# c as eight packed columns that TensorE spreads, and a column of ones that ties the first tiles' work behind the first dot

## The chip, the cores and the metric

The kernel runs on one core of one Trainium2 chip, in one launch. A core has five engines that run their own instruction streams: TensorE (PE in the rows, with its weight loads as PEld), VectorE (DVE), ScalarE (ACT), GpSimd (POOL) and SyncE (SP, which here issues most DMAs). They are held together by semaphores: an instruction waits until what it reads is written and what it overwrites has been read. The metric is the device time of one execution in microseconds (us), smaller is better.

## The reference

The model is a trunk of two mixer layers, each followed by a gated MLP with a width-3 convolution, on 1024 tokens of 1024 channels in f32. Every sub-layer is normalised and modulated by a vector that is computed from one conditioning row c of 1024 numbers. Cut to what the change touches:

```python
c_act = jax.nn.silu(c)
for i in range(DEPTH):
    mod = c_act @ mod_w[i] + mod_b[i]
    sh_a, sc_a, g_a, sh_f, sc_f, g_f = [t[:, None, :] for t in jnp.split(mod, 6, axis=-1)]
    h = rms_norm(x) * (1 + sc_a) + sh_a
    ...
        proj = h @ w_in
        cq, ckv, k_rope = jnp.split(proj, [512, 768], axis=-1)
```

So nothing of the first projection can be multiplied before the scales (1 + sc_a) of its channels are there, and these are dot products of silu(c) with 1024 rows of mod_w.

## The kernel before, in words

Everything is stored with channels on the 128 partitions: x is eight tiles k of 128 channels by 1024 tokens, and the tokens are worked on in two halves of 512. Every f32 matrix product is made of three reduced-precision ones: each operand is split into a high part (ScalarE copies it to the narrower type) and a low part (VectorE subtracts), and `mm3` (L171) multiplies the weight's high part by that of x (L175), the weight's high by x's low (L176) and the weight's low by x's high (L177). In the profile's rows the first operand behind the arrow is the moving one.

The change lies in the first stage, the input projection of the first half. Its inner dimension is the eight channel tiles k. For each k three things are loaded: 128 rows of mod_w (tile `sraw`, 512 KB), 128 rows of the projection weight (tile `wraw`, 448 KB) and a tile of x (256 KB); `load_k` issues the three, and `load_x` the last. `prepare(k)` then does, in this order: VectorE's dot of the mod_w rows with the row `crow` (`mod_dot`, L198, which writes one column of `modc`), the bias on that column (`mod_bias`, L203), ScalarE's high part of the weight (`winh`, L339), the high part of x times the scale column (`scaled`, L347, tile `h`), VectorE's low part of the same (L348), and the low part of the weight (`winl`, L341). `in_k` lets TensorE multiply the tile into seven PSUM accumulators `ia`, 21 matmuls for each k, 168 in all. Beside it ScalarE squares each x tile (L236, L239) and VectorE adds the squares (L241); after the last tile TensorE sums them over partitions (`st`, L250), VectorE makes the variance (`var`, L254), GpSimd the power -0.5 (`rstd`, L255), and TensorE spreads the result over rows (`rb`, L262). The accumulators are read out with that result.

`crow` is silu(c) on all 128 partitions. Before, a DMA writes c to every partition (L134, 128 rows of 4 KB) and ScalarE applies Silu to the 128x1024 tile (L135). Constants that are needed as columns lie packed in `cols`, 124 columns in its first part, loaded by one DMA (L156) in `load_k(0)`. Until the first real matmul TensorE runs 14 matmuls of 128x128 on the identity (`warm`, L405); each is shown as two records.

In the same stage stand the tables for the rotary embedding (`rope_tables`: four small loads of the positions into the tile `rt`, seventeen small operations on ScalarE and VectorE), further dots with loaded rows (`row`, the tiles `row` of mod_w), and the loads and splits of the second half of x.

The order of the instructions on each engine is not the order of the source: a scheduler of the framework orders them ahead of time from the program, its dependences and its own estimates, except where `tc.high_priority()` or `tc.keep_in_program_order` stand. So an edit at the start can shift what stands where on each engine in the first stage; the order below shows where.

## Time and profile before

| | us |
|---|---|
| three runs | 2194.0, 2195.18, 2199.16 |
| median of the three | 2195.18 |
| the profiled execution, its own time | 2196.67 |
| span of that execution in the trace | 2194.9 |
| TensorE busy | 2164.6 (99%) |
| VectorE busy | 1692.5 (77%) |
| ScalarE busy | 1049.7 (48%) |
| mean granted TensorE clock | 0.994 |

Times in the trace count from the start of the span. The span is from the first to the last instruction that the profiler records; 1.77 us of the execution lie around it. Matmuls are pipelined, so the busy time of TensorE counts a matmul as busy from its start to its modelled end; the granted clock tells how fast it was allowed to run (1.00 is 2.4 GHz, 0.50 is 1.2 GHz). In a row of the timeline the bracket tells how long the engine had stood idle before the instruction and what it waited for. Idle time of an engine that nobody waits for costs nothing.

### The profile page before, as it was taken

What the parts mean: (1) busy time and instruction counts of PE and PEld (TensorE: products, weight loads), DVE (VectorE), ACT (ScalarE), POOL (GpSimd) and SP (SyncE); (2) the same over time, 40 slices, a digit from 0 to 9 for tenths busy, and PEclk for the clock granted to TensorE, in tenths of its full rate; (3) what the DMA queues carried; (4) which work ended last, traced back from release to release, by engine and by line L of the source; (5) the groups of instructions that cost most, each with busy time, mean ns of one, the idle gap of its engine ahead of it and who ended that gap; (6) DMA issues with size and microseconds to landing.
All of it is one profiled execution on the core that took longest, in us unless ns stands there. A gap on an engine that the chain in (4) does not pass through costs nothing.

```text
span 2194.9 us, 28739 instructions
## 1 busy us (share of the span) xinstructions
PE 2164.6 (99%) x10557; PEld 1818.9 (83%) x10557; DVE 1692.5 (77%) x2769; ACT 1049.7 (48%) x1812; POOL 175.2 (8%) x216
## 2 busy tenths in 40 slices
PE   9999999999999999999999999999999999999998
PEld 7878888787888888878888888988788888887887
DVE  8877878669878777899973655566897777779997
ACT  6465566446544444443454434354554444453335
POOL 0000000000000000042210111010000000002232
PEclk9999999999999999999999999999999999999999
DMA  8512334831444332642132233444243333245122
GB/s 317 151 51 62 93 105 146 284 129 68 158 139 136 124 123 92 206 151 88 53 122 92 59 125 115 130 151 176 68 144 101 111 109 103 72 158 194 64 80 77
DMA packets 105085, 270.50 MB, mean 123 GB/s; under 512 B 12336, under 2 KB 15984, under 8 KB 104944
## 3 DMA queue, kind: packets, MB, share of 16 engines
q1 hardware_dynamic: 104544, 268.28, 37.2%
q8 instruction: 83, 1.36, 0.3%
q14 instruction: 58, 0.48, 0.1%
q10 hardware_dynamic: 400, 0.39, 0.1%
HBM read 221.53 MB, written 44.47 MB: 121 GB/s over the span
## 4 chain that ended last, share of the span: by engine, by line
PE 84%; DVE 9%; DMA 2%; ACT 2%; issue 2%; POOL 0%; SPq 0%; DVEq 0%; POOLq 0%; ACTq 0%
PE pa L175 7%; PE pa L177 7%; PE pa L176 7%; PE sc L673 3%; PE pd L177 3%; PE pd L175 3%; PE pd L176 3%; PE db L175 3%; PE db L176 3%; PE db L177 3%; PE op L175 3%; PE op L176 3%; PE op L177 3%; PE da L175 2%; PE da L176 2%; PE da L177 2%
## 5 line engine op out<-in xcount | busy, mean ns | idle before, releaser
L988 ACT ACTIVATE whi<-raw 128x512 fp32r<-128x512 f32 (+1 forms) x252 | 147.9, 608 | 248.3 <-PE pb L176 61.0
L988 ACT ACTIVATE whi<-wsum 128x512 fp32r<-128x512 f32 (+1 forms) x224 | 134.3, 619 | 177.4 <-PE pa L176 61.5
L175 PE MATMUL pa<-T,whi 128*128 128x512 f32 x528 | 205.9, 390 | 0.0
L176 PE MATMUL pa<-T,whi 128*128 128x512 f32 x528 | 205.4, 389 | 0.0
L177 PE MATMUL pa<-T,wlo 128*128 128x512 f32 x528 | 205.1, 389 | 0.0
L989 DVE TENSOR_TENSOR wlo<-wsum,whi 128x512 fp32r<-128x512 f32 (+1 forms) x224 | 151.5, 692 | 33.0 <-ACT whi L988 31.6
L989 POOL TENSOR_TENSOR wlo<-raw,whi 128x512 fp32r<-128x512 f32 (+1 forms) x80 | 116.3, 1467 | 401.2 <-ACT whi L988 398.7
L177 PE MATMUL da<-U,wlo 128*128 128x512 f32 (+1 forms) x364 | 138.4, 383 | 2.0 <-DVE wlo L989 2.0
L175 PE MATMUL da<-U,whi 128*128 128x512 f32 (+1 forms) x364 | 139.3, 383 | 0.4 <-DVE x L294 0.4
L176 PE MATMUL da<-U,whi 128*128 128x512 f32 (+1 forms) x364 | 139.2, 382 | 0.0
L989 DVE TENSOR_TENSOR wlo<-raw,whi 128x512 fp32r<-128x512 f32 (+1 forms) x172 | 116.1, 681 | 24.9 <-ACT whi L988 24.9
L167 ACT ACTIVATE whi<-wraw 128x1024 fp32r<-128x1024 f32 x67 | 70.8, 1060 | 117.5 <-PE op L176 59.3
L175 PEld LDWEIGHTS pa<-T,whi 128*128 128x128 f32 x528 | 99.1, 188 | 22.4 <-ACT whi L988 1.2
L177 PEld LDWEIGHTS pa<-T,wlo 128*128 128x128 f32 x528 | 99.1, 188 | 20.6
L176 PEld LDWEIGHTS pa<-T,whi 128*128 128x128 f32 x528 | 99.1, 188 | 20.2
L1028 ACT ACTIVATE ct<-a,cols 128x512 f32<-128x512 f32 x88 | 71.1, 812 | 83.7 <-DVE a L1050 47.8
L1140 DVE TENSOR_TENSOR U<-q,U 128x1024 fp32r<-128x1024 f32 x84 | 102.7, 1239 | 10.3 <-ACT U L1139 9.8
L168 DVE TENSOR_TENSOR wlo<-wraw,whi 128x1024 fp32r<-128x1024 f32 x67 | 81.7, 1222 | 29.8 <-ACT whi L167 27.7
L175 PE MATMUL db<-U,whi 128*128 128x512 f32 x264 | 103.3, 391 | 1.3 <-ACT whi L988 1.3
L177 PE MATMUL db<-U,wlo 128*128 128x512 f32 x264 | 102.8, 389 | 0.0
L176 PE MATMUL db<-U,whi 128*128 128x512 f32 x264 | 102.8, 389 | 0.0
L175 PE MATMUL inp<-h,whi 128*128 128x512 f32 x256 | 100.9, 395 | 0.0
(378 smaller groups left out, 6079.4 us busy)
## 6 DMA issues: line engine op xcount, KB each, us to landing
raw<-in_wf SPq DMA_DIRECT2D x96, 512.0 KB, 4.1
wraw<-in_w SPq DMA_DIRECT2D x67, 512.0 KB, 3.6
mraw<-in_mod_w SPq DMA_DIRECT2D x56, 512.0 KB, 3.9
ud<-ct SPq DMA_DIRECT2D x88, 256.0 KB, 2.3
q<-ud SPq DMA_DIRECT2D x88, 256.0 KB, 4.3
raw<-in_wd SPq DMA_DIRECT2D x32, 512.0 KB, 6.0
pa<-in_mod_w SPq DMA_DIRECT2D x24, 512.0 KB, 3.7
x<-xd SPq DMA_DIRECT2D x48, 256.0 KB, 4.7
```

The lines of the kernel that those rows point to most:

```text
L167: act.activation(hi, raw, AF.Copy)
L168: dve.tensor_tensor(lo, raw, hi.bitcast(F32), ALU.subtract)
L175: pe.matmul(ps, lh, rh, start=first, stop=False, skip_group_check=more)
L176: pe.matmul(ps[:, 0:rl.shape[-1]], lh, rl, start=False, stop=False, skip_group_check=more)
L177: pe.matmul(ps, ll, rh, start=False, stop=last, skip_group_check=more)
L673: pe.matmul(ps[:, cs], a[:, qs if n < 3 else qrs_], b[:, cs], start=n == 0, stop=n == 4)
L988: act.activation(hi, src, AF.Copy)
L989: eng.tensor_tensor(lo, src, hi.bitcast(F32), ALU.subtract)
L1028: act.activation(t, a[:, 2:], AF.Identity, bias=col(f"cb{l}", m), scale=cw(m, 2))
L1140: dve.tensor_tensor(lo, w, hi.bitcast(F32), ALU.subtract)
```

## The change

The broadcast load of c and the Silu on 128x1024 go. c is stored as eight columns of 128 in `cols`, which thereby has 132 columns in its first part, and that load is now the first one issued. ScalarE applies Silu to the eight columns (`ccol`); TensorE transposes each column, read as 128 equal columns, with the identity, four into one PSUM tile `cr` and four into another; VectorE copies the two tiles into the halves of `crow`, at high priority. The warming matmuls become 4 before the transposes and 5 after them. The first x tile is issued by ScalarE's queue instead of SyncE's. `load_k(0)`, `load_k(1)` and `prepare(0)` now stand ahead of `rope_tables` in the source.

`one` is a column of 128 ones that VectorE computes as 0 times the first scale column plus 1, so it exists only after the first dot and its bias. It is given as the scalar operand of the dots k = 1 to 3, as the scale of the high parts of the weight k = 1 to 3 and of the squares k = 0 to 3, and it is copied into the tile that the positions are loaded into, ahead of their loads. No value changes by it. The low part of the first weight tile is kept in program order.

```diff
@@ -40,7 +40,7 @@
 
 STEPS = "nspppnspppoooonmooso", "nnsposppooponpmspoopo"
 XW = (4, 2)
-WARM = 14
+WARM, WARM2 = 4, 5
 W0, W0_RSTD, WF, WF_RSTD = (6, 10), (4, 3), (4, 5), (4, 4)
 SHARE = 7
 GATES = (2, 18, 22, 26)
@@ -61,7 +61,7 @@
 
 
 
-_W = [("mb0", 48), ("mb1", 48), ("qn", 4), ("kvn", 2), ("hn", 8), ("fn", 8), ("invf", 1), ("mg", 3), ("gb", 2),
+_W = [("mb0", 48), ("mb1", 48), ("qn", 4), ("kvn", 2), ("hn", 8), ("fn", 8), ("invf", 1), ("mg", 3), ("gb", 2), ("c", 8),
       ("cw0", 66), ("cb0", 22), ("cw1", 66), ("cb1", 22)]
 COL = {}
 _o = 0
@@ -131,8 +131,6 @@
 
 
     crow = cst.tile([P, D], F32, name="crow")
-    nc.sync.dma_start(crow, c_d.broadcast_to([P, D]))
-    act.activation(crow, crow, AF.Silu)
     cols = [cst.tile([P, COLS[0][1]], F32, name="cols"), None, None]
     ident = cst.tile([P, P], F32, name="ident")
     make_identity(nc, ident)
@@ -194,8 +192,8 @@
             e[1]()
 
 
-    def mod_dot(l, i, raw, c=None):
-        return dve.scalar_tensor_tensor(raw, raw, 1.0, crow if c is None else c, ALU.mult, ALU.mult, accum_out=modc[l][:, i:i + 1])
+    def mod_dot(l, i, raw, c=None, one=1.0):
+        return dve.scalar_tensor_tensor(raw, raw, one, crow if c is None else c, ALU.mult, ALU.mult, accum_out=modc[l][:, i:i + 1])
 
     def mod_bias(l, i, n=1):
 
@@ -318,7 +316,7 @@
     us = [[(p0w if k < INNER else p0).tile([P, 896], F32R, name=f"win{j}{k}") for j in "hl"] for k in range(KT)]
 
     def load_x(hf, k):
-        nc.sync.dma_start(xs[hf][:, k, :], xT[k, :, hf * HS:(hf + 1) * HS])
+        (act if hf + k == 0 else nc.sync).dma_start(xs[hf][:, k, :], xT[k, :, hf * HS:(hf + 1) * HS])
 
     def small(name):
         return psS.tile([P, HS], F32, tag="sm", bufs=1, name=nm(name))
@@ -326,19 +324,21 @@
     def load_k(k):
 
         nc.sync.dma_start(sraw[:, k % 4, :], mod_w[0, 8 + k])
-        if k == 0:
-            load_cols(0, cst)
         nc.sync.dma_start(wraw[:, k % 4, :], win[k])
         load_x(0, k)
 
     def prepare(k):
         hi, lo = us[k]
         raw = wraw[:, k % 4, :]
-        mod_dot(0, 8 + k, sraw[:, k % 4, :])
+        mod_dot(0, 8 + k, sraw[:, k % 4, :], one=one if 0 < k < 4 else 1.0)
         mod_bias(0, 8 + k)
-        act.activation(hi, raw, AF.Copy)
+        act.activation(hi, raw, AF.Copy, scale=one if 0 < k < 4 else 1.0)
+        if k == 0:
+            dve.tensor_scalar(one, modc[0][:, 8:9], 0.0, 1.0, ALU.mult, ALU.add)
         scaled(0, k)
-        dve.tensor_tensor(lo, raw, hi.bitcast(F32), ALU.subtract)
+        i = dve.tensor_tensor(lo, raw, hi.bitcast(F32), ALU.subtract)
+        if k == 0:
+            tc.keep_in_program_order(i)
 
     def scaled(hf, k):
 
@@ -362,6 +362,7 @@
 
         Q = S // 4
         ang, n, n1, n2, t, pi = [scr[:, i * Q:(i + 1) * Q] for i in range(6)]
+        dve.tensor_copy(pi[:, 0:1], one)
         pi = pi.bitcast(I32)
         for i in range(4):
             nc.sync.dma_start(pi[32 * i:32 * i + 32, :], pos[:, i * Q:(i + 1) * Q].broadcast_to([32, Q]))
@@ -400,19 +401,33 @@
         rstd_later(ssq[hf], D, ssq[hf], keep_rb, XW[hf], small)
 
 
+    load_cols(0, cst)
+    load_k(0)
+    load_k(1)
     ps = small("warm")
     for _ in range(WARM):
         pe.matmul(ps[:, 0:P], ident, ident, start=True, stop=True)
 
-
-    load_k(0)
-    load_k(1)
+    ccol = cst.tile([P, KT], F32, name="ccol")
+    act.activation(ccol, cols_at(COL["c"], KT), AF.Silu)
+    for i in range(2):
+        cr = mm_tile("cr")
+        for t in range(4):
+            pe.transpose(cr[:, t * P:(t + 1) * P], ccol[:, i * 4 + t:i * 4 + t + 1].to_broadcast([P, P]), ident)
+        with tc.high_priority():
+            dve.tensor_copy(crow[:, i * HS:(i + 1) * HS], cr)
+    for _ in range(WARM2):
+        pe.matmul(ps[:, 0:P], ident, ident, start=True, stop=True)
+
+    one = cst.tile([P, 1], F32, name="one0")
+    prepare(0)
+
+
     cs_d = rope_tables(block(1, [P, 6 * 256], F32, "rt"))
     load_k(2)
     load_k(3)
-    prepare(0)
     accA = in_acc()
-    ssq[0].add(xs[0][:, 0, :])
+    ssq[0].add(xs[0][:, 0, :], scale=one)
 
     rows, shrow, inb = [], None, cst.tile([P, 7], F32, name="inb")
 
@@ -460,7 +475,7 @@
             h[1] = [block(4 + i, [P, KT, HS], F32R, "h") for i in range(2)]
             scaled(1, 0)
         if k < KT - 1:
-            ssq[0].add(xs[0][:, k + 1, :])
+            ssq[0].add(xs[0][:, k + 1, :], scale=one if k < 3 else 1.0)
         for r in ROWS_A[k]:
             row(r)
         if k == KT - 2:
@@ -1717,6 +1732,7 @@
     invf = np.array(INVF, f)
     put("invf", np.tile(invf, 4)[:, None])
     put("mg", np.tile(np.array([[MAGIC, -MAGIC, math.pi / 2]], f), (P, 1)))
+    put("c", _cols(a["c"][0]))
     put("gb", np.repeat(a["ml_b_gates"][0].reshape(2, MH).T, NC, axis=0))
 
     wi = a["mla_w_in"][0]
```

TensorE at the program's start. Names with a number are tiles; `ia` are accumulators, `warm` the warming matmuls, `cr` the spread c. Before:

```order
L405 MATMUL warm_116<-ident 128x128 x14
L175 MATMUL ia_174<-h_94,winh_98 128x512
L176 MATMUL ia_174<-h_95,winh_98 128x512
L177 MATMUL ia_174<-h_94,winl_99 128x512
L175 MATMUL ia_175<-h_94,winh_98 128x512
```

and now:

```order
L409 MATMUL warm_121<-ident 128x128 x4
L416 MATMUL cr_128<-ident,ccol 128x128 x4
L416 MATMUL cr_134<-ident,ccol 128x128 x4
L420 MATMUL warm_121<-ident 128x128 x5
L173 MATMUL ia_184<-h_92,winh_96 128x512
L173 MATMUL ia_185<-h_92,winh_96 128x512
L173 MATMUL ia_186<-h_92,winh_96 128x512
```

Before, the first accumulator gets its three products, then the second its three; now the high-by-high product comes first for one accumulator after another. Behind the rows shown there are seven of them in all before the others follow; L173, L174 and L175 now are L175, L176 and L177 of before.

ScalarE at the program's start, `x` with its number being the first half of x and `winh` with different numbers those of k = 0, 1, 2. Before:

```order
L135 ACT_TABLE_LOAD
L135 ACTIVATE crow<-crow 128x1024
L339 ACTIVATE winh_98<-wraw_97 128x896
L347 ACTIVATE h_94<-x_93,modc_79 128x512
L236 ACTIVATE ssq_114<-x_93 128x512
L339 ACTIVATE winh_100<-wraw_97 128x896
L347 ACTIVATE h_94<-x_93,modc_79 128x512
L239 ACTIVATE sq_195<-x_93 128x512
L368 ACTIVATE rt_138<-rt_138,cols 128x256
```

and now:

```order
L319 DMA x_91<-in_xT 128x512
L412 ACT_TABLE_LOAD
L412 ACTIVATE ccol<-cols 128x8
L335 ACTIVATE winh_96<-wraw_95 128x896
L347 ACTIVATE h_92<-x_91,modc_77 128x512
L234 ACTIVATE ssq_112<-x_91,one_145 128x512
L335 ACTIVATE winh_98<-wraw_95,one_145 128x896
L237 ACTIVATE sq_205<-x_91,one_145 128x512
L335 ACTIVATE winh_100<-wraw_95,one_145 128x896
L347 ACTIVATE h_92<-x_91,modc_77 128x512
L237 ACTIVATE sq_238<-x_91,one_145 128x512
```

The tile numbers of the two builds differ by two: the second tile's `winh_100` of before is `winh_98` now, and `winh_100` now is the third tile's. The squares of the second tile and the weight's high part of the third now stand ahead of the second `h`, where before the second `h` came directly behind the second `winh`. The first rotary operation (`rt_138`) stood ninth in the first piece, and it stands behind the rows shown in the second.

VectorE ahead of the first variance (`var`). `h_459` and `h_469` belong to the second half of x (`x_291`, `x_301`), `ssq_115` are the squares of that half, `row_310` to `row_314` dots with rows of mod_w. Before:

```order
L348 SCALAR_TENSOR_TENSOR h_459<-x_291,modc_79,h_458 128x512
L348 SCALAR_TENSOR_TENSOR h_95<-x_93,modc_79,h_94 128x512
L348 SCALAR_TENSOR_TENSOR h_459<-x_291,modc_79,h_458 128x512 x3
L241 TENSOR_TENSOR ssq_115<-ssq_115,sq_582 128x512
L241 TENSOR_TENSOR ssq_115<-ssq_115,sq_585 128x512
L348 SCALAR_TENSOR_TENSOR h_459<-x_291,modc_79,h_458 128x512
L241 TENSOR_TENSOR ssq_115<-ssq_115,sq_588 128x512
L254 TENSOR_SCALAR var_438<-st_433 128x4
```

and now:

```order
L239 TENSOR_TENSOR ssq_112<-ssq_112,sq_412 128x512
L196 SCALAR_TENSOR_TENSOR row_310,modc_77<-row_310,crow 128x1024
L348 SCALAR_TENSOR_TENSOR h_93<-x_91,modc_77,h_92 128x512
L201 SCALAR_TENSOR_TENSOR modc_77<-modc_77,cols 128x1
L196 SCALAR_TENSOR_TENSOR row_312,modc_77<-row_312,crow 128x1024
L196 SCALAR_TENSOR_TENSOR row_314,modc_77<-row_314,crow 128x1024
L201 SCALAR_TENSOR_TENSOR modc_77<-modc_77,cols 128x1
L348 SCALAR_TENSOR_TENSOR h_469<-x_301,modc_77,h_468 128x512
L252 TENSOR_SCALAR var_448<-st_443 128x4
```

Before, five low parts and three sums of squares of the second half stand ahead of the variance in the rows shown; now three dots on rows with two biases, one such low part, and the rest behind it.

## Rows read from the trace of the kernel before

**Rows 1.** The page, first part: busy time of each engine, its share of the span, and its instructions.
```profile
PE 2164.6 (99%) x10557; PEld 1818.9 (83%) x10557; DVE 1692.5 (77%) x2769; ACT 1049.7 (48%) x1812; POOL 175.2 (8%) x216
```

**Rows 2.** Busy time by stretch, whole core. Columns: the stretch, its length, then for PE, PEld, DVE, ACT and POOL the busy time and instructions, then the granted TensorE clock (1.00 is full), the DMA engines' busy share, and GB/s.
```profile
0.00:10.00 10.00, 6.01 (x29) 5.78 (x29) 2.45 (x5) 4.39 (x5) 0.78 (x8) 0.99 0.79 274
10.00:20.00 10.00, 9.72 (x30) 7.38 (x30) 8.71 (x17) 8.33 (x15) 0.00 (x0) 0.67 1.04 380
20.00:40.00 20.00, 20.00 (x90) 16.57 (x89) 19.70 (x37) 12.69 (x22) 0.00 (x0) 1.00 0.82 291
40.00:60.00 20.00, 19.95 (x97) 16.14 (x96) 19.09 (x38) 8.79 (x15) 1.85 (x1) 1.00 0.83 308
```

**Rows 3.** The timeline of the first 13 us. Columns: start in us, length in us, engine, line, operation, output<-input, shapes, count, and in brackets how long the engine had stood idle and what released it.
```profile
1.46 5.69 PE L405 MATMUL warm<-ident 128*128 128x128 f32 x28 [1.46 <-POOL ident masks.py:199]
...
5.08 1.06 ACT L135 ACTIVATE crow<-crow 128x1024 f32<-128x1024 f32 x1 [3.01 <-DMA crow<-in_c]
6.74 1.23 DVE L198 SCALAR_TENSOR_TENSOR sraw<-sraw,crow 128x1024 f32<-128x1024 f32 x1 [6.74 <-DMA sraw<-in_mod_w]
...
7.96 0.95 ACT L339 ACTIVATE winh<-wraw 128x896 fp32r<-128x896 f32 x1 [1.81 <-DMA wraw<-in_win]
...
8.90 0.72 ACT L347 ACTIVATE h<-x,modc 128x512 fp32r<-128x512 f32 x1
...
9.68 0.79 PE L175 MATMUL ia<-h,winh 128*128 128x512 f32 x1 [2.54 <-ACT h L347]
9.95 0.75 DVE L348 SCALAR_TENSOR_TENSOR h<-x,modc,h 128x512 fp32r<-128x512 f32 x1
...
10.75 0.79 PE L176 MATMUL ia<-h,winh 128*128 128x512 f32 x1 [0.28 <-DVE h L348]
...
11.34 0.63 PE L177 MATMUL ia<-h,winl 128*128 128x512 f32 x1
...
11.44 0.95 ACT L339 ACTIVATE winh<-wraw 128x896 fp32r<-128x896 f32 x1 [1.29 <-DMA wraw<-in_win]
...
11.77 0.63 PE L175 MATMUL ia<-h,winh 128*128 128x512 f32 x1
...
12.61 0.73 ACT L347 ACTIVATE h<-x,modc 128x512 fp32r<-128x512 f32 x1 [0.22 <-DMA x<-in_xT]
```

**Rows 4.** Half-microsecond stretches of the start, columns as in rows 2.
```profile
2.00:2.50 0.50, 0.50 (x5) 0.50 (x4) 0.00 (x0) 0.08 (x1) 0.00 (x0) 1.00 0.87 319
6.50:7.00 0.50, 0.50 (x6) 0.45 (x5) 0.26 (x1) 0.00 (x0) 0.00 (x0) 1.00 1.09 376
9.50:10.00 0.50, 0.32 (x1) 0.29 (x1) 0.50 (x2) 0.50 (x2) 0.00 (x0) 0.72 0.97 390
16.50:17.00 0.50, 0.50 (x4) 0.42 (x3) 0.08 (x1) 0.50 (x2) 0.00 (x0) 0.96 0.96 384
```

**Rows 5.** The timeline where the first normaliser is made, columns as in rows 3.
```profile
44.64 0.94 PE L250 MATMUL st<-ones,ssq 128*128 128x1 f32 x8
...
45.62 0.16 DVE L254 TENSOR_SCALAR var<-st 128x4 f32<-128x4 f32 x1 [0.36 <-PE st L250]
...
45.94 1.85 POOL L255 TENSOR_TENSOR rstd<-var,nhalf 128x4 f32<-128x4 f32 x1 [44.53 <-DVE var L254]
...
47.85 0.65 PE L262 MATMUL rb<-ident,rstd 128*128 128x128 f32 x4
```

**Rows 6.** Groups of VectorE's instructions in the first 46 us: line, engine, operation, shapes, count | busy us, mean ns of one | idle time just before them and what ended it.
```profile
L198 DVE SCALAR_TENSOR_TENSOR sraw<-sraw,crow 128x1024 f32<-128x1024 f32 x8 | 9.8, 1222 | 6.7 <-DMA sraw<-in_mod_w 6.7
L348 DVE SCALAR_TENSOR_TENSOR h<-x,modc,h 128x512 fp32r<-128x512 f32 x13 | 9.6, 748 | 0.7 <-ACT h L347 0.7
L341 DVE TENSOR_TENSOR winl<-wraw,winh 128x896 fp32r<-128x896 f32 x8 | 8.7, 1089 | 1.2 <-ACT winh L339 1.2
L241 DVE TENSOR_TENSOR ssq<-ssq,sq 128x512 f32<-128x512 f32 x10 | 6.9, 687 | 0.1
...
L374 DVE TENSOR_TENSOR rt<-rt 128x256 f32<-128x256 f32 x1 | 0.4, 426 | 0.8 <-ACT rt L373 0.8
...
L254 DVE TENSOR_SCALAR var<-st 128x4 f32<-128x4 f32 x1 | 0.2, 164 | 0.4 <-PE st L250 0.4
```

**Rows 7.** The same for ScalarE, two of its groups.
```profile
L347 ACT ACTIVATE h<-x,modc 128x512 fp32r<-128x512 f32 x15 | 10.6, 718 | 3.7 <-DVE modc L203 2.9 <-DMA x<-in_xT 0.8
...
L239 ACT ACTIVATE sq<-x 128x512 f32<-128x512 f32 x12 | 7.3, 618 | 1.9 <-DMA x<-in_xT 1.9
```

**Rows 8.** DMA issues of the first 40 us: output<-input, queue, operation, count, KB each, median us from issue to landing.
```profile
crow<-in_c SPq DMA_DIRECT2D x1, 512.0 KB, 4.3
...
cols<-in_cols SPq DMA_DIRECT2D x1, 62.0 KB, 5.1
```

**Rows 9.** TensorE's waits in the stretch with its largest loss of time (timeline, columns as in rows 3), and behind them two stretches of it (columns as in rows 2).
```profile
112.82 0.50 PE L175 MATMUL qrp<-cqn,whi 128*128 128x512 f32 x1 [0.61 <-ACT cqn L495]
113.93 0.50 PE L176 MATMUL qrp<-cqn,whi 128*128 128x512 f32 x1 [0.61 <-DVE cqn L496]
...
116.59 0.79 PE L175 MATMUL kp<-ckvn,whi 128*128 128x512 f32 x1 [1.93 <-ACT ckvn L495]
...
116.00:118.00 2.00, 1.41 (x5) 1.29 (x6) 1.30 (x3) 1.75 (x3) 0.00 (x0) 0.50 0.52 117
...
122.00:124.00 2.00, 2.00 (x11) 1.83 (x10) 0.72 (x4) 0.00 (x0) 0.00 (x0) 0.91 0.00 0
```

## The prediction

> **What bounds the kernel now.** I read the page's first part before anything else [rows 1]: TensorE is busy 99% of the span, 2164.6 of 2194.9 us, so some 30 us in all are left in which it stands. The change touches only the start, so the next views are the busy times by stretch and the timeline of the first microseconds [rows 2, 3]. The reader is to see there what the start costs TensorE: 1.46 us until the identity exists, 2.54 us between the warming matmuls and the first real one, 0.28 us ahead of the second. The third matmul comes at 11.34, although at the pitch of the half clock (from 11.34 to the next start, 11.77, are 0.43 us, 512 columns at 1.2 GHz) it could have come at 9.68 + 2 x 0.43 = 10.54: 0.8 us more. VectorE is idle until 6.74 and then as busy as TensorE: 8.71 of 10 us, 19.70 of 20, 19.09 of 20 [rows 2]. That is the sentence that decides here: in this stage two engines are full, and the one that ends last at the stage's end counts.
>
> The stage ends where the normaliser goes back to TensorE [rows 5]: sums on TensorE, the variance on VectorE at 45.62, GpSimd's power at 45.94 for 1.85 us, the spreading on TensorE at 47.85. From the variance's start to the spreading are 2.23 us. The variance had waited only 0.36 us for TensorE's sums, so VectorE was through with all ahead of it at 45.26. Between the sums and the spreading TensorE has matmuls of its own, so a later or an earlier TensorE moves the stage by less than one thinks: from 47.85 on it is VectorE's queue that sets the time.
>
> **The row c.** What goes: the 512 KB load, 4.3 us to its landing [rows 8], and the Silu of 1.06 us from 5.08. The dot came at 6.74, when its own weights had landed, 0.6 us after the row [rows 3]. What comes: `cols` issued first. Its landing is bounded by the row's 4.3 us above, and below by the same less the transfer of the bytes that are gone (0.45 MB at 319 GB/s [rows 4], 1.4 us): 2.9 to 4.3 us after 0.80, so 3.7 to 5.1; I take 3.7, as the load is small. Silu on 8 columns: the rows show 1.06 us for 1024 columns and 0.62 for 512 [rows 3, 7]; the difference puts 8 columns near 0.2, bounds 0 and 0.62, I take 0.3. Eight transposes: four take 0.65 us [rows 5], so 1.3; at the pitch of the warming records (5.69/28 = 0.20 each) 1.6. The last copy to `crow` at 0.7 (a VectorE pass over 512 columns takes 0.69 to 0.75 [rows 6]); the first lies beside the second four transposes. Handovers are 0.16 us where rows show one (0.16 from the variance's end to the power's start [rows 5]). Sum: 3.7 + 0.3 + 1.3 + 0.7 + 3 x 0.16 = 6.5; bounds 5.9 and 5.1 + 0.62 + 1.6 + 0.75 + 0.5 = 8.6. The weights of the first dot have 0.32 MB ahead of them (`cols` and x) instead of 0.52, worth 0.5 us at 376 GB/s [rows 4], so 6.2. The later of the two sets the dot: 6.5, 0.25 us earlier than before.
>
> **The first matmuls.** Before, TensorE waited for `winh` at 7.96 (its load) and then `h`: 9.68 [rows 3]. The load has 0.27 MB less ahead of it, 0.7 us, so `winh` starts near 7.25; the scale is there at 6.5 + 1.23 + 0.24 = 8.0; `h` follows at 8.2, and 0.78 us after its start the first matmul (as from 8.90 to 9.68): about 8.95, 0.75 us earlier. The 0.28 and the rest of the 0.8 go as well, since seven high-by-high matmuls (3.0 us at 0.43) now stand ahead of the ones that need the low parts: VectorE makes the low part of x by about 11.0 and that of the weight by 12.1, and the seven end at 11.95. TensorE's lead is then 0.75 + 0.8 = 1.55 us. The warming matmuls cost nothing: five of them, ten records of 0.20, run behind the transposes and end near 5.6 + 2.0 = 7.6, when TensorE has nothing else to do; without that cover their 2.0 us would be lost.
>
> x(0) on ScalarE's queue is ahead of the weights of the first dot rather than behind: 0.25 MB at 376 GB/s, 0.7 us, if they share the engines; the DMAs are already 0.79 to 1.09 busy in these stretches [rows 2, 4], so I have put it into the 0.32 MB above. The Trainium skill ("DMA: Bandwidth & Descriptors", section "Issuing engines are not separate DMA queues") speaks against that edit: loads started by several engines run on the same 16 engines and interleave, and only the issuing time is saved. By this rule it gains only the issuing time of one load and gives 0.7 us back at the dot; no row of before shows a load from that queue at the start.
>
> **VectorE up to the variance.** Work: of the second half of x, four low parts less (4 x 0.748) and three sums less (3 x 0.687) stand ahead of the variance, and three row dots (3 x 1.222) and two biases more; with `one` and its copy these four small ones are 4 x 0.164, the variance's own duration being the nearest row [rows 5, 6]. -2.99 - 2.06 + 3.67 + 0.66 = -0.72 us. A column as the operand of the dot costs 0 to 0.1 (ScalarE's pass with such a column takes 0.718, without it 0.618 [rows 7]); three times that is inside the spread.
>
> Idle: before, after the start, 0.7 + 1.2 + 0.8 = 2.7 us, for ScalarE's `h`, `winh` and `rt` [rows 6]. The 1.2 for `winh` goes, for the low part of the weight comes later now. In its place the second dot stands directly behind the first and waits for its weights, from 8.3 to about 8.9 (0.98 MB behind the first dot's, 2.6 to 2.8 us at 345 to 376 GB/s after 6.2): 0.6. And ScalarE makes the third weight's high part ahead of the second `h`; that weight has 3.54 MB up to its end, 2.7 more than the first dot's weights at 6.2; at 345 to 380 GB/s (the second is the row of 10 to 20 us, the first what lies between 6.74 and the x load that ended at 12.61, 2.0 MB) it lands at 13.3 to 14.0. Then 0.95 and 0.72: the second `h` is there at 15.0 to 15.7, against 13.3 before. VectorE reaches its low part at about 14.0 with two low parts of the weight and one sum done: it waits 1.0 to 1.7. With the 0.7 and 0.8 that stay: 3.1 to 3.8, 0.4 to 1.1 more than before.
>
> So VectorE is through at 45.26 - 0.25 - 0.72 + (0.4 to 1.1) = 44.7 to 45.4, and the spreading can start 2.23 later, at 46.9 to 47.6 against 47.85: 0.2 to 0.9 us gained, 0.6 taken. The other 0.95 of TensorE's lead becomes waiting ahead of the spreading; what ScalarE's ties (`one` as scale) hold back is held behind a dot that they came after in the rows of before too, so they cost nothing while that dot is not late. The position loads go from their place behind the second tile to one behind the fourth; their four issues no longer stand ahead of the third tile's loads, and the rotary work that hangs on them has cover on ScalarE and is needed far later.
>
> **The sum.** 2196.67 - 0.6 = 2196.1 for an execution like the profiled one, whose span is 2194.9 with 1.77 around it; it lies 1.49 above the median of 2195.18, so the forecast is 2194.6, its own range 2193.6 to 2195.7 (from a gain of 1.55, all of TensorE's lead, to a loss of 0.5, the runs' scatter aside).
>
> **The rivals.** A: VectorE isn't the gate, and TensorE's whole lead goes through. For it: the variance's 0.36 us of waiting for TensorE. Against it: the sum above. And the clock: it was shown full until about 9.7, half from there to about 16.5, after 2.54 us without matmuls [rows 2 to 4]; half of 6.8 us is 3.4 us lost. An earlier and denser start could bring that back in part, say half: 1.55 + 1.7 = 3.3, so 2195.18 - 3.3 = 2191.9. The Trainium skill ("TensorE: Matmul & The Clock Gate", Part 1) says that the point of the rise varies from run to run with where the first matmuls fall; the rows here show one execution and can't tell how much.
>
> B: the largest later loss, 112 to 122 us, shrinks. TensorE waits 0.61 + 0.61 + 1.93 there, and the clock stands at half [rows 9]: 3.15 us and some 3.4 for the clock. If VectorE comes there relatively earlier and the clock doesn't fall, up to 6.5 go: 2195.18 - 0.6 - 6.5 = 2188.1. Against it: the order behind the first stage is the same, and what counts there is how far VectorE and ScalarE are ahead of TensorE, not when all of them began.
>
> C, slower: ScalarE's new order makes the second `h` so late that VectorE's queue ends after 45.62 and TensorE waits at the spreading beyond 47.85. The point from which it decides is 1.3 us more idle time than before at VectorE (45.62 less 44.29); 2.1 more (the third weight landing at 15.0) cost 0.8, and if TensorE in that pause loses the clock for half as long as at the start, 3.4 us, 1.7 more: 2195.18 + 2.5 = 2197.7. The `cols` load at its upper bound (dot at 8.6, 1.9 late) ends in the same place.
>
> D: the change doesn't do what it says, because the row c wasn't what the dot waited for: the dot waited for its own weights [rows 3], and with `cols` landing at 4.0 the row is there at 6.8. Then the start stays as it is and the order gives and takes: 2195.2.
>
> **Chances.** The forecast 0.55, A 0.12, B 0.05, C 0.16, D 0.12. What a measurement of this kernel can tell from no change is about 0.3%, 6.6 us; only B with a part of A, or a loss several times that of C, reach beyond it. Faster 0.06, same 0.89, slower 0.05. The range for 8 in 10 takes in A and C and, as three runs of before scatter over 5 us, a little beyond: 2191 to 2198.3.
>
> **What would show it.** Right: the first dot at 6.2 to 6.7 and no broadcast load; the first matmul near 9.0 with seven of its kind behind it; VectorE waiting for the second `h` near 15; the spreading at 46.9 to 47.6 with TensorE waiting about 1 us ahead of it; the same three waits near 112 us. Wrong: the dot after 7.0 (the row's path mis-sized); the spreading later than 47.85 (C); full clock before 14 us or through 112 to 122 (A, B).

## The result and the profile after

The changed kernel takes 2205.35 us (median of 6 runs, 2202.56 to 2206.9) beside 2195.64 for the kernel before in the same runs: ratio 1.0033, 95% interval 1.0023 to 1.0043. It is slower by 5 to 9 us, and the forecast, no change with a small gain, was wrong. The profiled execution took 2204.81, span 2203.1.

The page's first part, which answers to [rows 1]:

```profile
PE 2172.8 (99%) x10555; PEld 1815.6 (82%) x10555; DVE 1693.2 (77%) x2773; ACT 1046.7 (48%) x1812; POOL 177.7 (8%) x216
```

The span grew by 8.2 us and TensorE's busy time by 8.2 (2172.8 against 2164.6). So TensorE waits no longer than before in all; its matmuls themselves take longer. The start by stretch, columns as in [rows 2]:

```profile
0.00:10.00 10.00, 6.53 (x28) 6.01 (x29) 3.98 (x8) 3.68 (x5) 0.78 (x8) 1.00 0.82 298
10.00:20.00 10.00, 9.87 (x42) 7.30 (x40) 8.48 (x15) 7.07 (x12) 0.00 (x0) 1.00 1.04 386
20.00:40.00 20.00, 19.34 (x82) 15.38 (x83) 19.00 (x36) 13.16 (x24) 0.00 (x0) 1.00 0.86 319
40.00:60.00 20.00, 19.16 (x93) 15.24 (x92) 18.81 (x39) 6.96 (x13) 2.59 (x1) 1.00 0.86 323
```

The granted clock is 1.00 (2.4 GHz) from 10 to 20 us, where it was 0.67, and 42 matmul records stand there instead of 30. But from 20 to 40, at the same full clock, there are 82 instead of 90, with 19.34 us busy: fewer matmuls in nearly the same time. The timeline of the start, which answers to [rows 3]:

```profile
4.30 0.21 ACT L412 ACTIVATE ccol<-cols 128x8 f32<-128x8 f32 x1 [1.77 <-DMA cols<-in_cols]
...
4.57 1.97 PE L416 MATMUL cr<-ident,ccol 128*128 128x128 f32 x8 [1.02 <-ACT ccol L412]
...
6.57 0.69 DVE L418 COPY crow<-cr 128x512 f32<-128x512 f32 x1 [0.16 <-PE cr L416]
...
7.30 1.23 DVE L196 SCALAR_TENSOR_TENSOR sraw<-sraw,crow 128x1024 f32<-128x1024 f32 x1
...
9.53 1.90 PE L173 MATMUL ia<-h,winh 128*128 128x512 f32 x7 [0.98 <-ACT h L347]
...
12.45 1.05 ACT L335 ACTIVATE winh<-wraw,one 128x896 fp32r<-128x896 f32 x1 [0.80 <-DMA wraw<-in_win]
...
14.14 0.75 DVE L348 SCALAR_TENSOR_TENSOR h<-x,modc,h 128x512 fp32r<-128x512 f32 x1 [0.50 <-ACT h L347]
```

And the first normaliser, which answers to [rows 5]:

```profile
44.48 0.16 DVE L252 TENSOR_SCALAR var<-st 128x4 f32<-128x4 f32 x1
44.79 2.59 POOL L253 TENSOR_TENSOR rstd<-var,nhalf 128x4 f32<-128x4 f32 x1 [43.38 <-DVE modc L201]
...
47.44 0.65 PE L260 MATMUL rb<-ident,rstd 128*128 128x128 f32 x4 [0.84 <-POOL rstd L253]
```

The spreading starts at 47.44, 0.41 earlier than before, with TensorE waiting 0.84 us ahead of it. So the stage that the change touches went about as forecast. To see where the time went, the same instructions of ScalarE are set side by side along the run; the first of them, at 145 us, serves as the early marker in the experiments below. First those of before (timeline, columns as in [rows 3]), then those of after:

```profile
145.86 1.06 ACT L167 ACTIVATE whi<-wraw 128x1024 fp32r<-128x1024 f32 x1 [1.01 <-PE kp L176]
...
503.92 0.63 ACT L988 ACTIVATE whi<-wsum 128x512 fp32r<-128x512 f32 x1
...
1004.64 0.63 ACT L988 ACTIVATE whi<-raw 128x512 fp32r<-128x512 f32 x1 [3.10 <-DVE raw L1173]
...
2001.02 0.64 ACT L988 ACTIVATE whi<-raw 128x512 fp32r<-128x512 f32 x1 [3.07 <-DVE raw L1173]
```

```profile
145.39 1.06 ACT L165 ACTIVATE whi<-wraw 128x1024 fp32r<-128x1024 f32 x1 [1.00 <-PE kp L174]
...
503.18 0.62 ACT L1003 ACTIVATE whi<-wsum 128x512 fp32r<-128x512 f32 x1
...
1008.69 0.63 ACT L1003 ACTIVATE whi<-raw 128x512 fp32r<-128x512 f32 x1 [3.13 <-DVE raw L1188]
...
2009.29 0.63 ACT L1003 ACTIVATE whi<-raw 128x512 fp32r<-128x512 f32 x1 [3.05 <-DVE raw L1188]
```

After is 0.47 us ahead at 145 us, 0.74 ahead at 504, 4.05 behind at 1005 and 8.27 behind at 2001. It loses its time in the two MLPs (about 500 to 980 and 1540 to 1960 us), where instructions and order are those of before. Two stretches within them, before and then after (columns as in [rows 2]):

```profile
700.00:900.00 200.00, 200.00 (x884) 165.68 (x883) 152.66 (x247) 90.76 (x149) 0.80 (x8) 1.00 0.35 112
1700.00:1900.00 200.00, 200.00 (x884) 165.61 (x883) 147.00 (x239) 87.54 (x147) 1.00 (x10) 1.00 0.31 101
```

```profile
700.00:900.00 200.00, 200.00 (x875) 164.00 (x874) 150.38 (x244) 89.28 (x147) 0.80 (x8) 1.00 0.35 111
1700.00:1900.00 200.00, 200.00 (x875) 164.06 (x874) 145.53 (x235) 88.17 (x148) 1.10 (x11) 1.00 0.31 102
```

TensorE never stands, its clock is full, and 875 matmuls take the time of 884. Which ones are slower is told by TensorE's groups from 500 to 980 us (line, operation, shapes, count | busy us, mean ns of one | idle), before and then after:

```profile
L177 PE MATMUL pd<-B,wlo 128*128 128x512 f32 x88 | 34.1, 389 | 0.0
...
L177 PE MATMUL pa<-h,wlo 128*128 128x512 f32 x78 | 30.3, 389 | 0.0
```

```profile
L175 PE MATMUL pd<-B,wlo 128*128 128x512 f32 x88 | 34.8, 397 | 0.0
...
L175 PE MATMUL pa<-h,wlo 128*128 128x512 f32 x77 | 30.0, 389 | 0.0
```

Matmuls of one shape, from one instruction in the source: those that stream tile B became 8 ns slower, those that stream tile h didn't. A piece of after's timeline on TensorE shows it as a pitch, the time from one start to the next:

```profile
719.93 0.39 PE L173 MATMUL pa<-T,whi 128*128 128x512 f32 x1
...
722.04 0.39 PE L173 MATMUL pb<-h,whi 128*128 128x512 f32 x1
...
722.74 0.39 PE L173 MATMUL pb<-h,whi 128*128 128x512 f32 x1
...
723.42 0.39 PE L173 MATMUL pb<-h,whi 128*128 128x512 f32 x1
```

Nine matmuls on T take 2.11 us (0.234 each), three on h 0.68 (0.227). The three on h directly behind those on T, from 722.04 to 722.74, still take 0.70.

### The profile page after: what moved, and what is told of

The parts are those of the page before. It is cut to its first block, busy times and chain, and to the rows that moved or that the text cites. A ratio compares the mean times of both kernels' runs of the same rounds, so it can differ in the third digit from the quotient of the medians.

```text
span 2203.1 us, 28723 instructions
## 1 busy us (share of the span) xinstructions
PE 2172.8 (99%) x10555; PEld 1815.6 (82%) x10555; DVE 1693.2 (77%) x2773; ACT 1046.7 (48%) x1812; POOL 177.7 (8%) x216
## 4 chain that ended last, share of the span: by engine, by line
PE 82%; DVE 11%; DMA 4%; ACT 2%; issue 1%; SPq 0%; POOL 0%; DVEq 0%; POOLq 0%; ACTq 0%
PE pa L175 7%; PE pa L173 7%; PE pa L174 7%; PE pd L175 3%; PE sc L688 3%; PE pd L174 3%; PE pd L173 3%; PE op L173 3%; PE op L174 3%; PE op L175 2%; PE da L173 2%; PE da L174 2%; PE db L173 2%; PE inp L175 2%; PE da L175 2%; PE db L174 2%
## 5 line engine op out<-in xcount | busy, mean ns | idle before, releaser
L174 PE MATMUL pa<-T,whi 128*128 128x512 f32 x528 | 206.9, 392 | 0.0
L173 PE MATMUL pa<-T,whi 128*128 128x512 f32 x528 | 206.9, 392 | 0.0
L175 PE MATMUL pa<-T,wlo 128*128 128x512 f32 x528 | 206.7, 392 | 0.0
L175 PE MATMUL da<-U,wlo 128*128 128x512 f32 (+1 forms) x364 | 138.4, 383 | 2.0 <-DVE wlo L1004 2.0
L173 PE MATMUL da<-U,whi 128*128 128x512 f32 (+1 forms) x364 | 139.3, 383 | 0.7 <-DVE x L292 0.7
L174 PE MATMUL da<-U,whi 128*128 128x512 f32 (+1 forms) x364 | 139.2, 382 | 0.0
L173 PEld LDWEIGHTS pa<-T,whi 128*128 128x128 f32 x528 | 99.2, 188 | 23.6 <-ACT whi L1003 0.8
L174 PEld LDWEIGHTS pa<-T,whi 128*128 128x128 f32 x528 | 99.3, 188 | 21.7
L175 PEld LDWEIGHTS pa<-T,wlo 128*128 128x128 f32 x528 | 99.1, 188 | 21.7
L1155 DVE TENSOR_TENSOR U<-q,U 128x1024 fp32r<-128x1024 f32 x84 | 102.6, 1238 | 10.2 <-ACT U L1154 9.7
L173 PE MATMUL db<-U,whi 128*128 128x512 f32 x264 | 103.3, 391 | 1.3 <-ACT whi L1003 1.3
L175 PE MATMUL db<-U,wlo 128*128 128x512 f32 x264 | 103.0, 390 | 0.2 <-DVE wlo L1004 0.2
L174 PE MATMUL db<-U,whi 128*128 128x512 f32 x264 | 102.8, 389 | 0.0
L174 PE MATMUL inp<-h,whi 128*128 128x512 f32 x256 | 101.0, 395 | 0.4 <-DVE h L276 0.4
```

Source lines behind the costliest of these rows:

```text
L173: pe.matmul(ps, lh, rh, start=first, stop=False, skip_group_check=more)
L174: pe.matmul(ps[:, 0:rl.shape[-1]], lh, rl, start=False, stop=False, skip_group_check=more)
L175: pe.matmul(ps, ll, rh, start=False, stop=last, skip_group_check=more)
L1155: dve.tensor_tensor(lo, w, hi.bitcast(F32), ALU.subtract)
```

## The experiments

**The theory.** What these tiles have in common is their place. Tiles are allocated from the two ends of the on-chip memory, called its two sides here; the distance of two tiles is the difference of their start addresses. The change adds three things to the constants: 8 columns of 4 bytes in `cols`, the tile `ccol` of 8 columns, and `one`, which takes a step of 32 bytes: 96 bytes in all. In the build every tile allocated behind them on that side of the on-chip memory lies 96 bytes further: the streamed x, h, U and most of the T (streamed means read as the moving operand), and all split weights of the later stages. The tiles of the other side stay: the first stage's split weights (`winh`, `winl`), the MLP's streamed B and one of its T. In the build of before the distance between a streamed tile and its weights is a multiple of 256 bytes in all large pairs; now pairs from two different sides lie 96 bytes nearer to each other, and the tiles that became slow belong to such pairs. The rival: schedule, that is, the new order, ScalarE's load or the denser start makes later matmuls slow.

In what follows the edit is mostly one line, for `n` unused columns of 4 bytes in a constant tile:

```diff
-    modc = [cst.tile([P, 48], F32, name=f"modc{i}") for i in range(2)]
+    modc = [cst.tile([P, 48 + n * i], F32, name=f"modc{i}") for i in range(2)]
```

**The kernel before, moved by 96 bytes** (`n` = 24, nothing else).

> The kernel before with one constant tile 96 bytes wider (24 unused columns), which moves every tile allocated behind it on that side of the on-chip memory by 96 bytes, as the change did; the instructions and their order are those of before. Layout theory: the loss is where the operands lie, not what the change does, so this alone gives the slow matmuls: pd<-B at 395 to 397 ns instead of 389 to 390, about 875 matmuls in 700 to 900 us instead of 884, and 2204 to 2207 us. Schedule theory (the new order, the second DMA queue or the denser start makes the later matmuls slow): the same as before, 2194 to 2198, 884 matmuls.

Measured: 2208.44 us (4 runs), ratio 1.0052, interval 1.0035 to 1.0068. A group and a stretch of it:

```profile
L177 PE MATMUL pd<-B,wlo 128*128 128x512 f32 x88 | 34.8, 397 | 0.0
```

```profile
700.00:900.00 200.00, 200.00 (x875) 163.99 (x874) 150.77 (x245) 89.38 (x149) 0.90 (x9) 1.00 0.34 111
```

With the instructions and the order of before, both are after's numbers; the time is 1.4 above the 2207 expected at most. The address alone makes such a loss; schedule is out.

**The unit.** Three runs asked which distance counts: the changed kernel with `n` = 8 (128 bytes against before), the kernel before with `n` = 16 (64), and the changed kernel with the other side moved too:

```diff
-    stT, pt = phase("tab", side="right")
+    ctx.enter_context(tc.tile_pool(name="edge", bufs=1, side="right")).tile([P, 24], F32, name="edge"); stT, pt = phase("tab", side="right")
```

> The changed kernel with the same tile 32 bytes wider, so that the shift against before is 128 bytes instead of 96. Layout theory with a unit of 64 or 128 bytes: the matmuls are fast again (389 to 390 ns for pd<-B, 884 in 700 to 900 us), and the change shows its own worth: 2192 to 2196 us. Layout theory with a larger unit, or schedule theory: 2203 to 2207 as the changed kernel.

> The kernel before with the tile 64 bytes wider. Layout theory with a unit of 64 bytes: as before, pd<-B 389 to 390 ns, about 2195 us. With a unit of 128 bytes or more: slow, pd<-B 395 to 397, about 2205. Schedule theory: as before.

> The changed kernel with the tiles of the other side of the memory moved by 96 bytes as well, so that all tiles have moved alike and the distances between the two sides are those of before. If what counts is how two operands lie to each other: fast, pd<-B 389 to 390 ns, 884 matmuls in 700 to 900 us, about 2195 us. If it is where each tile lies by itself (behind a multiple of 64 bytes): every matmul slow, over 2205 us. Schedule theory: 2203 to 2207.

All three stayed slow: 2203.15 us (10 runs, ratio 1.003, interval 1.002 to 1.0039), 2206.43 and 2205.7 (one run each), with 876, 874 and 876 matmuls from 700 to 900 us. Units of 64 and 128 bytes fell. The last text was wrong about its own edit: a tile added to that side pushes the others down, toward the first side, so the two sides were 192 bytes nearer and not alike. Read so, the runs leave one simple rule for a stage as a whole: a multiple of 256.

Not every group follows it. In the run with 192 bytes, TensorE's groups from 500 to 980 us read

```profile
L173 PE MATMUL pd<-B,whi 128*128 128x512 f32 x88 | 34.8, 396 | 0.0
...
L174 PE MATMUL pd<-B,whi 128*128 128x512 f32 x88 | 34.4, 390 | 0.0
...
L173 PE MATMUL pb<-h,whi 128*128 128x512 f32 x80 | 31.6, 395 | 0.0
```

One of the three products on B is as fast as before, and a product on h is slow, although h and its weights lie on one side and have moved alike. In the stretch at 722.74 us of that run twelve matmuls on h, directly behind slow ones on T, take 2.77 us (0.231 each). So the slower pitch can carry over to matmuls behind the pairs that crossed the sides; why, no run shows.

**Moved by 256 bytes.** The changed kernel with `n` = 40, the kernel before with `n` = 64, and the changed kernel with 40 columns in the `edge` tile, so that 96 from one side and 160 from the other make 256 while every tile lies at a place of its own.

> The changed kernel with the constant tile 160 bytes wider, so that the shift against before is 256 bytes. The four runs so far say that a matmul is fast when the distance between what it streams and the weights loaded beside it is a multiple of 256 bytes, as in all large pairs of before, and slow at 64, 96, 128, 160 or 192 beyond. By that rule: pd<-B back at 389 to 390 ns, 884 matmuls in 700 to 900 us, and the change alone is left: 2193 to 2196 us, at or up to 3 below before, no longer above it. If the change had a cost of its own behind the start: 2198 or more. If the unit is larger than 256 (512): slow, 2203 or more.

> The kernel before shifted by 256 bytes. Rule of 256: no change, 2194 to 2199 us and 389 to 390 ns for pd<-B. A rule by which each tile's own place counts, or one of 512: slow, 2204 or more.

> The changed kernel with the tiles of the other side moved by 160 bytes toward the first, so that each tile lies elsewhere than before, and the distance between the two sides is 256 less than before (the earlier run with 96 on the other side moved the two toward each other too, by 192 in all, and not alike as its text said). Rule of the distance: fast, 389 to 390 ns, 2193 to 2197 us. Rule of each tile's own place (both sides now at a multiple of 64): slow, 2203 or more.

All three are fast: 884 matmuls from 700 to 900 us, and 389 to 390 ns for pd<-B. The first, 160 bytes beside the changed kernel:

```profile
L175 PE MATMUL pd<-B,wlo 128*128 128x512 f32 x88 | 34.1, 389 | 0.0
```

Its time is 2196.42 us (11 runs; at most 2196 was expected) beside 2197.3 for before: ratio 0.9996, interval 0.9987 to 1.0005. The others took 2197.03 and 2195.29 (one run each). It is the distance that counts, not each tile's place, and 160 unused bytes give back all that the change lost (ratio 0.9996 instead of 1.0033, 8 us). What is left of the change can't be told from no change.

**The least step, and one pair alone.** The kernel before with `n` = 8, and the kernel before with two streamed tiles of the MLP (B, and the one of pa's three T that lies on its side) moved by 96 bytes:

```diff
             T[n] = t[:, 0:4], t[:, 4:8]
-        rstd_later(ssq, D, T["T1"], lambda rb: operands_second(px, xs, rb, l, T), X_WAIT[1], up_ps,
+        px.tile([P, 24], F32, name=nm("edge")); rstd_later(ssq, D, T["T1"], lambda rb: operands_second(px, xs, rb, l, T), X_WAIT[1], up_ps,
```

> The kernel before shifted by 32 bytes, the least step of the allocation. Rule of 256: slow, with pd<-B between 391 and 397 ns and 2200 to 2207 us; the size at this distance isn't known from the runs so far (at 64 beyond the multiple it was 393 to 396). If distances up to 32 bytes are forgiven: as before.

> The kernel before with only two of the MLP's four streamed operand tiles (those of pd<-B and a quarter of pa<-T) moved by 96 bytes; the weights, the other operands and the first stage stay. Rule of the distance: the first 500 us as before, then 4 us lost in each MLP (500 to 980 and 1540 to 1960 us), pd<-B at 395 to 397 ns, the others at 389 to 391; 2202 to 2206 us in all. If the weights' own place counts: as before.

32 bytes are enough: 2211.23 us in one run (4 above the 2207 expected at most), 874 matmuls from 700 to 900, 396 ns for pd<-B. With the two tiles alone it is 2203.72 in one run, and its groups from 500 to 980 us read

```profile
L177 PE MATMUL pd<-B,wlo 128*128 128x512 f32 x88 | 34.8, 397 | 0.0
...
L177 PE MATMUL pa<-h,wlo 128*128 128x512 f32 x78 | 30.3, 389 | 0.0
```

with the early marker where it was before, against 2 us later when all was moved by 96; first this kernel, then that one:

```profile
145.69 1.06 ACT L167 ACTIVATE whi<-wraw 128x1024 fp32r<-128x1024 f32 x1 [1.01 <-PE kp L176]
```

```profile
147.76 1.06 ACT L167 ACTIVATE whi<-wraw 128x1024 fp32r<-128x1024 f32 x1 [1.00 <-PE kp L176]
```

So some 2 us of the loss by address belong to the first stage (its weights lie on the other side), and some 7 us (this single run beside 2196.75) to these two tiles; what is left of the 11.5 us by which the kernel moved as a whole is behind isn't traced. Set together, by how much nearer the two sides lie than before (matmuls from 700 to 900 us, mean ns of the three pd<-B groups):

| bytes | kernel | matmuls | pd<-B, ns |
|---|---|---|---|
| 0 | before | 884 | 389 to 390 |
| 32 | before, n = 8 | 874 | 396 |
| 64 | before, n = 16 | 874 | 395 |
| 96 | changed; before, n = 24 | 875 | 395 to 397 |
| 128 | changed, n = 8 | 876 | 394 to 395 |
| 192 | changed, edge of 24 | 876 | 390 to 396 |
| 256 | changed, n = 40; before, n = 64; changed, edge of 40 | 884 | 389 to 390 |

**The parts of the change, with the layout of 256.** The ties are the uses of `one`, which keep work of the first tiles behind the first dot. Without the ties:

```diff
-        mod_dot(0, 8 + k, sraw[:, k % 4, :], one=one if 0 < k < 4 else 1.0)
+        mod_dot(0, 8 + k, sraw[:, k % 4, :], one=1.0)
...
-            dve.tensor_scalar(one, modc[0][:, 8:9], 0.0, 1.0, ALU.mult, ALU.add)
+            pool.memset(one, 1.0)
...
-        dve.tensor_copy(pi[:, 0:1], one)
+        pass
```

and 1.0 for `one` at the other scales. With the ties but the row as before:

```diff
+    nc.sync.dma_start(crow, c_d.broadcast_to([P, D]))
+    act.activation(crow, crow, AF.Silu)
...
-WARM, WARM2 = 4, 5
+WARM, WARM2 = 14, 0
```

with the Silu on columns, the transposes and the copies left out, and the first x still on ScalarE's queue.

> The changed kernel shifted by 256 bytes and without the ties: the column of ones is set at once and used nowhere, so the scheduler is free with the first tiles. In its order VectorE makes the low part of the second weight and the second squares ahead of the copies of the row c, and ScalarE the first rotary operations and three weights ahead of the first h. If the ties hold what they were meant to hold, the first dot waits for the second weight (near 10 us), the first matmul comes near 14 us instead of 9.5, and the time is 3 to 6 us above the run with 160 bytes. If they only cost, it is the same or below.

> The changed kernel shifted by 256 bytes, with the row c made as before (broadcast load first, Silu on 128x1024, 14 warming matmuls at once, no transposes), and with the ties and the first x on ScalarE's queue kept. The row's load and x then both stand ahead of the first dot's weights: dot near 7.4 us, first matmul near 10.2 (9.4 in the run with 160 bytes), the clock falls to half as in before. By 126 us it should be 1 to 2 us behind the run with 160 bytes, so at or a little under before; in the time that is 2196 to 2199, not to be told from before. If the row's path is worth nothing, it is level with the run with 160 bytes at 126 us.

Without the ties it is 2206.01 us (5 runs, ratio 1.0039, interval 1.0026 to 1.0052). VectorE's first instruction is the second weight's low part, and TensorE starts at 16.56:

```profile
10.37 1.09 DVE L339 TENSOR_TENSOR winl<-wraw,winh 128x896 fp32r<-128x896 f32 x1 [10.37 <-ACT winh L335]
...
16.56 1.65 PE L173 MATMUL ia<-h,winh 128*128 128x512 f32 x3 [8.27 <-ACT h L347]
```

The early marker is at 153.95, 8.1 behind before; 9.6 us behind the run with 160 bytes in the time, more than the 3 to 6 expected. With the ties and the old row it is 2199.46 (10 runs, ratio 1.0016, interval 1.0006 to 1.0025), marker at 148.21, 2.35 behind. 2196 to 2199, not to be told from before, was expected. First dot 7.92, first matmul 10.57 (7.4 and 10.2 were expected), and TensorE then waits for VectorE's variance:

```profile
44.74 0.95 PE L250 MATMUL st<-ones,ssq 128*128 128x1 f32 x8
48.57 0.16 DVE L254 TENSOR_SCALAR var<-st 128x4 f32<-128x4 f32 x1
...
50.38 0.65 PE L262 MATMUL rb<-ident,rstd 128*128 128x128 f32 x4 [2.49 <-POOL rstd L255]
```

The new row without the ties is a loss, and so are the ties with the old row; both together are 1.7 us ahead at the marker (144.15). What the ties cost by themselves isn't shown, since the run with the old row also has x on ScalarE's queue.

**The first x back on SyncE**, layout of 256:

```diff
-        (act if hf + k == 0 else nc.sync).dma_start(xs[hf][:, k, :], xT[k, :, hf * HS:(hf + 1) * HS])
+        nc.sync.dma_start(xs[hf][:, k, :], xT[k, :, hf * HS:(hf + 1) * HS])
```

> The changed kernel shifted by 256 bytes, with the first x tile issued by SyncE behind the first weight instead of by ScalarE; the rest of the change stays. In the run with 160 bytes the first dot came at 7.14, 0.7 us after the first copy of the row c had ended at 7.1, so it is the row's path that sets it and not the loads: dot near 7.1 and first matmul near 9.4 again, if x(0) has no part in it; the weights land some 0.5 us earlier, which nothing waits for. The order ahead of the variance changes too (two row dots and three low parts instead of three and one), the variance at 44.5 to 45.5. Time level with the run with 160 bytes, 2195 to 2198, and at or up to 2 us under before. If the place of x mattered as the rule of the shared engines has it: dot at 6.5 to 6.7, 0.5 us gained at the first matmul.

Measured: 2198.04 us (11 runs), ratio 0.9995, interval 0.9986 to 1.0004. The expectation of the start was wrong. (The copy of the row that ended at 7.1 in the run with 160 bytes is the second one, and the dot stood directly behind it.) Its rows, and then those of the run with x on ScalarE's queue:

```profile
2.80 0.21 ACT L412 ACTIVATE ccol<-cols 128x8 f32<-128x8 f32 x1 [0.72 <-DMA cols<-in_cols]
...
6.00 1.23 DVE L196 SCALAR_TENSOR_TENSOR sraw<-sraw,crow 128x1024 f32<-128x1024 f32 x1
...
8.99 1.28 DVE L196 SCALAR_TENSOR_TENSOR sraw<-sraw,one,crow 128x1024 f32<-128x1024 f32 x1 [1.18 <-DMA sraw<-in_mod_w]
...
47.51 0.65 PE L260 MATMUL rb<-ident,rstd 128*128 128x128 f32 x4 [1.38 <-POOL rstd L253]
```

```profile
4.15 0.21 ACT L412 ACTIVATE ccol<-cols 128x8 f32<-128x8 f32 x1 [1.60 <-DMA cols<-in_cols]
...
7.14 1.23 DVE L196 SCALAR_TENSOR_TENSOR sraw<-sraw,crow 128x1024 f32<-128x1024 f32 x1
...
46.73 0.65 PE L260 MATMUL rb<-ident,rstd 128*128 128x128 f32 x4 [0.55 <-POOL rstd L253]
```

Without the 256 KB of x beside it the 66 KB of `cols` are there 1.35 us sooner, the dot 1.14 sooner; and yet the spreading comes 0.78 later. Of that 0.78, GpSimd's power makes 0.40 (1.85 us instead of 1.45) and a later variance 0.38 (45.29 instead of 44.91). The second dot now waits 1.18 us for its weights, and VectorE's order ahead of the variance is another; which of the two makes the variance late wasn't separated. The early part agrees with the Trainium skill ("DMA: Bandwidth & Descriptors", section "Issuing engines are not separate DMA queues"): loads of several engines share the same 16 engines.

## Why the prediction was wrong, and where it was right

- **The step that failed** is the one that ended the sum with the start: the text put everything behind the first stage at nothing, and its only reason, given against rival B, is that "the order behind the first stage is the same". The order is; the addresses aren't. The term that was missing is the slower pitch of the matmuls whose operands lie on different sides, some 8 us by the run with 160 bytes. No rival had it: A to D moved waits or the clock, and the loss is in busy time at full clock. The same change without the shift took 2196.42, inside the range of 2191 to 2198.3 and 0.9 below before in the same runs, where 0.6 was forecast; neither can be told from no change.
- **The row c**: dot at 7.30, forecast 6.5. Two terms were too small. `cols` was there at 4.30 and not at 3.7, because I let x(0) delay the weights behind it but not `cols` beside it; and the eight transposes took 1.97, not 1.3. The text had named a dot after 7.0 as the sign of that.
- **The first matmuls**: 9.53, forecast 8.95. All seven high-by-high matmuls stood at once, as forecast. They ran at about 0.25 (1.90 us less the last one's 0.4, over six) and not at 0.43: the clock part of rival A came true, with TensorE idle for 0.98 us ahead of them instead of 2.54.
- **VectorE as the gate** held. The third weight landed at 12.45 rather than 13.3 to 14.0, so the second `h` was there at 14.1 rather than 15.0 to 15.7; VectorE waited 0.50 for it and not 1.0 to 1.7, and the variance came at 44.48, just ahead of the 44.7 to 45.4 forecast. GpSimd's power then took 2.59 instead of 1.85, so the spreading came at 47.44, within 46.9 to 47.6, with 0.84 us of waiting where about 1 was forecast. That it fell within is partly luck: the dot was 0.8 late and the power 0.74 longer, while VectorE's waits were shorter than forecast. TensorE's lead went into those 0.84 us, as the sum had it, into 0.77 us of waits for `h` at 20.4 and 21.2, and into the slower pitch of this stage's matmuls, which the sum didn't have. In the run with 160 bytes the power took 1.45 us and the spreading came at 46.73.
- **B**: the sign named for the forecast, the same three waits near 112 us, didn't hold. The wait of 0.61 for ScalarE's `cqn` was gone, the other 0.61 and the 1.93 stood, one of 0.20 was new, and the clock was higher there; first before, then after (columns as in [rows 2]):

```profile
112.00:122.00 10.00, 6.85 (x19) 4.91 (x19) 8.61 (x19) 6.53 (x12) 0.00 (x0) 0.68 0.29 79
```

```profile
112.00:122.00 10.00, 7.25 (x25) 4.94 (x24) 8.99 (x19) 6.51 (x12) 0.00 (x0) 0.83 0.27 79
```

  So B came true in a small part. The kernel before moved by 96 bytes has a clock of 0.78 there too, so it doesn't take the change for that.
- **C**, a VectorE so late that TensorE waits at the spreading beyond 47.85, didn't happen in this kernel. It did with ties and the old row, where TensorE waited 2.49 us, though not in C's way: VectorE waited only 0.19 us for the second `h` there.

Left open: whether the weights that count are a matmul's own or those loaded beside it, and why the slower pitch can carry over to the matmuls behind; distances of 160 and 224 bytes, and steps under 32, weren't tried; and what in the chip makes the unit of 256 bytes the runs don't show.

## What to carry to other kernels

A new constant of a few bytes can move every tile allocated behind it. After an edit look first at a stage that it doesn't touch: if TensorE's busy time grew by as much as the span and the same stretch holds fewer matmuls at the same clock, compare the tiles' addresses before the schedule. For back-to-back matmuls like these keep the distance between a streamed tile and its weights at a multiple of 256 bytes, with unused columns if need be, and judge the edit itself only then.

## What the runs showed of the hardware that was not expected

- A back-to-back matmul of 128x512 takes 227 ns from start to start when the tile that it streams and its weights lie a multiple of 256 bytes apart, and some 234 when they lie 96 off that, with the clock at 1.00 in both; 32 bytes are enough for the full loss (one run).
- GpSimd's power on a 128x4 tile took 1.44 to 2.59 us in these runs. TensorE stood 0.84 us ahead of the spreading in the changed kernel, where it took 2.59, and not at all in before, where it took 1.85; what sets its length no run shows.
- At the start, one 256 KB load on a second queue delayed a 66 KB load issued at the same time by 1.35 us (one profile of each).
